# An RMS norm that streams 67 MB: the first store to memory takes four rows per partition instead of one

## The chip, the cores and the metric

The kernel runs on one core of a Trainium2 chip, the other cores idle. The metric is the device time of one execution in microseconds (us), lower is better. "The profile" is one execution taken by the hardware profiler. Its span is about 1.8 us shorter than the device time. A run over 1.5% above the fastest of its kernel counts as slow (164.01 of the kernel before is one); ranges list it, ratios leave it out.

## The reference

```python
def reference(x, gamma):                       # x: 16 x 1024 x 512 float32, gamma: 512
    eps = 1e-5
    rms = np.sqrt(np.mean(x ** 2, axis=-1, keepdims=True) + eps)
    return (x / rms * gamma).astype(np.float32)
```

16,384 rows of 512 floats are read, each scaled by its own factor and by gamma, and written: 33.56 MB in, 33.55 MB out.

## The kernel before

The rows are cut into four tiles of 128 partitions x 32 rows. A row is 2 KB, so one partition's rows of a tile are 64 KB, contiguous in memory. Three SBUF slots hold the tiles, and tile 3 reuses slot 0. All transfers are issued by SyncE on one queue, in program order. The parts that matter (cuts are marked):

```python
    load(0, 0, 0, 8)                  # tile, slot, first row, end row
    nc.sync.dma_start(out=gamma_row, in_=gamma.unsqueeze(0))
    load(0, 0, 8, 16)
    load(0, 0, 16, 32)
    load(1, 1, 0, 16)
    load(1, 1, 16, 32)
    # ... (cut)
    groups = [
        (0, 0, 7, (7,), 3),           # tile, first row, rows, pieces of the square sums, POOL's share
        (0, 7, 9, (9,), 5),
        (0, 16, 16, (7, 9), 7),
        # ... (cut)
    ]
    # ... (cut)
    def transfers(t, g):              # called after each group
        if (t, g) == (0, 0):
            store(0, 0, 0, 1)         # the early store: the program's first
            load(2, 2, 0, 20)
        elif (t, g) == (0, 16):
            load(2, 2, 20, 32)
            store(0, 0, 1, 16)
            store(0, 0, 16, 32)
            load(3, 0, 0, 16)         # slot 0 again: waits for the stores of its rows
            load(3, 0, 16, 32)
        # ... (cut): store(1, 1, 0, 32), store(2, 2, 0, 32), store(3, 0, 0, 32)
```

In each group POOL scales its share of the rows and multiplies them by gamma. ACT and DVE do the same for the other rows.

## Time and profile before

| | before |
|---|---|
| device time, median (lowest to highest), 3 runs | 161.67 us (161.36 to 164.01) |
| span of the profile | 159.7 us |
| busy DVE / ACT / POOL | 70% / 67% / 69% |
| DMA packets' time, as a share of 16 engines' span | 98.1% |
| data packets per DMA engine in the early store | 8 of 2 KB |

Here the DMA share is full and no compute engine is, which means that the transfers set the time, as long as the next transfer is always issued before the last one has ended.

The trace records each DMA packet's duration, though no view prints it. Packets of one size nearly all take the same time (1213 ns for 32 KB), but just before some turns from loads to stores, some load packets take longer, up to 2.3 us. (The first loads are stretched too, in the first 6 us; that belongs to no turn, and is left out.) The stretch of a turn is the sum of each packet's duration minus the median of its size, over the packets around the turn, divided by 16 engines. It is known to a few hundredths of a us, since where "around" ends is a choice.

### The profile page before, as it was taken

What the parts mean: (1) busy time and instruction counts of PE and PEld (TensorE: products, weight loads), DVE (VectorE), ACT (ScalarE), POOL (GpSimd) and SP (SyncE); (2) the same over time, 40 slices, a digit from 0 to 9 for tenths busy, and PEclk for the clock granted to TensorE, in tenths of its full rate; (3) what the DMA queues carried; (4) which work ended last, traced back from release to release, by engine and by line L of the source; (5) the groups of instructions that cost most, each with busy time, mean ns of one, the idle gap of its engine ahead of it and who ended that gap; (6) DMA issues with size and microseconds to landing.
All of it is one profiled execution on the core that took longest, in us unless ns stands there. A gap on an engine that the chain in (4) does not pass through costs nothing.

```text
span 159.7 us, 260 instructions
## 1 busy us (share of the span) xinstructions
PE 2.0 (1%) x2; PEld 0.5 (0%) x2; DVE 111.0 (70%) x40; ACT 106.6 (67%) x106; POOL 110.3 (69%) x24
## 2 busy tenths in 40 slices
PE   0040000000000000000000000000000000000000
PEld 0000000000000000000000000000000000000000
DVE  0018098899798999999999999999999094000000
ACT  3071967976999998999899899989960970000000
POOL 1000951994999599999999999999999999000000
DMA  6999999999999899989999999996996996997993
GB/s 195 415 439 464 460 394 419 492 402 394 402 451 492 361 412 425 492 378 451 468 394 419 501 394 394 525 509 279 525 509 279 525 509 279 525 460 328 525 394 131
DMA packets 2164, 67.12 MB, mean 420 GB/s; under 512 B 242, under 2 KB 242, under 8 KB 371
## 3 DMA queue, kind: packets, MB, share of 16 engines
q1 hardware_dynamic: 2162, 67.11, 98.1%
q14 instruction: 2, 0.01, 0.0%
HBM read 33.56 MB, written 33.55 MB: 420 GB/s over the span
## 4 chain that ended last, share of the span: by engine, by line
POOL 46%; ACT 18%; DVE 12%; DMA 5%; POOLq 4%; issue 0%
POOL slot L108 24%; POOL slot L107 22%; DVE ss L95 9%; ACT slot L94 7%; ACT sq_psum L94 6%; DMA slot<-in_x_dram 5%; POOLq L203 4%; ACT slot L116 3%; DVE slot L120 3%; ACT ss L100 1%; ACT gamma_b L158 0%; DVE ss L101 0%; POOLq L107 0%
## 5 line engine op out<-in xcount | busy, mean ns | idle before, releaser
L107 POOL TENSOR_TENSOR slot<-slot,ss 128x3584 f32<-128x3584 f32 (+2 forms) x9 | 48.6, 5404 | 24.0 <-DVE ss L101 24.0
L108 POOL TENSOR_TENSOR slot<-slot,gamma_b 128x3584 f32<-128x3584 f32 (+2 forms) x9 | 61.4, 6825 | 0.7
L95 DVE TENSOR_REDUCE ss<-sq_psum 128x7 f32<-128x3584 f32 (+1 forms) x13 | 42.2, 3246 | 13.5 <-ACT sq_psum L94 13.5
L116 ACT ACTIVATE slot<-slot,ss 128x512 f32<-128x512 f32 x73 | 46.0, 707 | 4.7 <-DVE ss L101 4.7
L120 DVE TENSOR_TENSOR slot<-slot,gamma_psum 128x4608 f32<-128x4608 f32 (+3 forms) x10 | 40.3, 4038 | 4.4 <-ACT slot L116 4.4
L94 ACT ACTIVATE sq_psum<-slot 128x3584 f32<-128x3584 f32 (+1 forms) x13 | 34.6, 2659 | 6.2 <-DMA slot<-in_x_dram 5.5
L95 DVE TENSOR_REDUCE ss<-slot 128x9 f32<-128x4608 f32 x3 | 14.9, 4953 | 4.4 <-ACT slot L94 4.2
L95 DVE TENSOR_REDUCE ss<-sq_sbuf 128x5 f32<-128x2560 f32 x5 | 14.0, 2801 | 0.0
L94 ACT ACTIVATE slot<-slot 128x4608 f32<-128x4608 f32 x3 | 12.1, 4033 | 0.0
L94 ACT ACTIVATE sq_sbuf<-slot 128x2560 f32<-128x2560 f32 x5 | 11.6, 2322 | 0.0
L100 ACT ACTIVATE ss<-ss,eps_t 128x16 f32<-128x16 f32 (+2 forms) x9 | 2.7, 305 | 11.9 <-DVE ss L95 11.9
L101 DVE RECIPROCAL ss<-ss 128x16 f32<-128x16 f32 (+2 forms) x9 | 2.1, 235 | 0.4 <-ACT ss L100 0.4
L64 PE MATMUL gamma_psum<-gamma_row,ones_col 1*128 1x512 f32 x2 | 2.0, 1121 | 7.9 <-DMA gamma_row<-in_gamma_dram 7.9
L70 ACT ACT_TABLE_LOAD x1 | 1.3, 1283 | 1.1 <-PEq L192 1.1
L158 ACT COPY gamma_b<-gamma_psum 128x512 f32<-128x512 f32 x1 | 0.6, 566 | 0.0
L64 PEld LDWEIGHTS gamma_psum<-gamma_row,ones_col 1*128 1x128 f32 x2 | 0.5, 304 | 7.8 <-issue 7.8
L62 POOL MEMSET ones_col<- 1x128 f32 x1 | 0.2, 194 | 0.3 <-POOLq L192 0.3
L192 POOL MEMSET const-float32-0.0<- 128x1 f32 x1 | 0.1, 98 | 0.2 <-issue 0.2
L70 ACT ACTIVATE table<-eps_t 128x1 f32<-128x1 f32 x1 | 0.2, 203 | 0.0
L192 POOL MEMSET const-bfloat16-1.0<- 128x1 bf16 x1 | 0.1, 101 | 0.0
L192 POOL MEMSET const-uint8-127<- 128x1 uint8 x1 | 0.1, 101 | 0.0
L192 POOL MEMSET const-float32-1.0<- 128x1 f32 x1 | 0.1, 98 | 0.0
(1 smaller groups left out, 0.1 us busy)
## 6 DMA issues: line engine op xcount, KB each, us to landing
slot<-in_x_dram SPq DMA_DIRECT2D x5, 4096.0 KB, 20.8
slot<-in_x_dram SPq DMA_DIRECT2D x1, 5120.0 KB, 27.7
slot<-in_x_dram SPq DMA_DIRECT2D x2, 2048.0 KB, 9.4
out_dram<-slot SPq DMA_DIRECT2D x1, 4096.0 KB, 26.5
out_dram<-slot SPq DMA_DIRECT2D x1, 3840.0 KB
slot<-in_x_dram SPq DMA_DIRECT2D x1, 3072.0 KB, 12.9
out_dram<-slot SPq DMA_DIRECT2D x1, 256.0 KB, 15.9
out_dram<-slot SPq DMA_DIRECT2D x3, 28.1
```

Of the source, the lines that this page charges most:

```text
L64: nc.tensor.matmul(gamma_psum[:, 0], ones_col, gamma_row, start=True, stop=True)
L70: nc.scalar.activation(out=table, in_=eps_t, func=AF.Sqrt)
L94: nc.scalar.activation(out=sq[:, :m], in_=rows, func=AF.Square)
L95: nc.vector.tensor_reduce(out=ss[:, r : r + m, 0], in_=sq[:, :m], axis=mybir.AxisListType.X, op=OP.add)
L100: nc.scalar.activation(out=ss[:, :n, 0], in_=ss[:, :n, 0], func=AF.Sqrt, bias=eps_t, scale=1.0 / D)
L101: nc.vector.reciprocal(out=ss[:, :n, 0], in_=ss[:, :n, 0])
L107: nc.gpsimd.tensor_tensor(out=part, in0=part, in1=by_row, op=OP.mult)
L108: last = nc.gpsimd.tensor_tensor(out=part, in0=part, in1=gamma_b.to_broadcast([P, share, D]), op=OP.mult)
L116: nc.scalar.activation(out=x[:, g + r, :], in_=x[:, g + r, :], func=AF.Copy, scale=rstd[:, r])
L120: scaled = nc.vector.tensor_tensor(out=part, in0=part, in1=gamma_psum.to_broadcast([P, r1 - r0, D]), op=OP.mult)
L158: nc.scalar.copy(out=gamma_b[:, 0], in_=gamma_psum[:, 0])
L203: with _tile.TileContext(nc) as tc:
```

## The change

The early store takes rows 0 to 3 of each partition instead of row 0 alone, 1 MB instead of 256 KB, and the later one takes the rest. The intent is that finished rows leave sooner, in packets of 8 KB instead of 2 KB.

```diff
         if (t, g) == (0, 0):
-            store(0, 0, 0, 1)
+            store(0, 0, 0, 4)
             load(2, 2, 0, 20)
         elif (t, g) == (0, 16):
             load(2, 2, 20, 32)
-            store(0, 0, 1, 16)
+            store(0, 0, 4, 16)
             store(0, 0, 16, 32)
```

## The prediction

> **What bounds the kernel now.** The kernel normalises 16,384 rows of 512 floats: four tiles, t = 0 to 3, each of 32 rows for every one of the 128 partitions, in three SBUF slots (tile 3 reuses slot 0). I read the page's busy shares first, then its queue part.
>
> ```profile
> span 159.7 us, 260 instructions
> PE 2.0 (1%) x2; PEld 0.5 (0%) x2; DVE 111.0 (70%) x40; ACT 106.6 (67%) x106; POOL 110.3 (69%) x24
> ...
> q1 hardware_dynamic: 2162, 67.11, 98.1%
> ```
>
> Three engines are near 70%, none full. The last line is queue, packets, MB, share of the 16 DMA engines' span: their packets fill 98.1% of it. The other 1.9% of 159.7 is 3.0 us, and half of that is the start: in the stretches view the first 5 us have a DMA share of 0.68, so 5 x 0.32 = 1.6 us. Everything is read once and written once (33.56 + 33.55 MB), so the DMA queue sets the end.
>
> The page's "chain that ended last" names POOL for 46%. That is misleading here: the merged chain ends in a last piece of 5.64 us from 129.86, so at 135.5 us, which is the wait for the last multiplication before the last store can be issued; 24 us of pure transfer follow. Whether that chain matters depends on whether the queue is empty at 135.5. So I next read when transfers are issued, in the timeline of the issuing engine, and their times to landing, in the view of each tensor, narrowed to a short window about each issue.
>
> ```profile
> 0.74 0.38 SPq L45 DMA_DIRECT2D slot<-in_x_dram  x1
> 1.18 0.32 SPq L55 DMA_DIRECT2D gamma_row<-in_gamma_dram  x1
> 1.55 2.10 SPq L45 DMA_DIRECT2D slot<-in_x_dram  x4
> 27.19 0.35 SPq L49 DMA_DIRECT2D out_dram<-slot  x1
> 27.58 22.42 SPq L45 DMA_DIRECT2D slot<-in_x_dram  x2
> 50.12 5.46 SPq L49 DMA_DIRECT2D out_dram<-slot  x2
> 71.64 10.41 SPq L45 DMA_DIRECT2D slot<-in_x_dram  x2
> 83.47 52.39 SPq L49 DMA_DIRECT2D out_dram<-slot  x3
> ```
>
> The store at 27.19 is the one that changes. Issue plus time to landing gives the queue's schedule. The first five loads land by 42.5 (3.2 + 39.3); the early store at 43.1 (27.2 + 15.9); tile 2's first 20 rows at 55.3 (27.6 + 27.7); its last 12, issued at 49.7, at 62.6; the store of rows 1 to 15 at about 71.6, since the load that waits for it goes out at 71.64; the store of rows 16 to 31 at 81.7; tile 3's two loads at 91.0 and 100.9; the three big stores at 120.3, 139.6 and 158.9. At every issue something earlier has not landed yet. The backlog is 42.5 - 27.2 = 15.3 us at the early store, 55.3 - 49.7 = 5.6 at tile 2's second load, 81.7 - 71.6 = 10.1 at tile 3's first, 120.3 - 111.5 = 8.8 at the store of tile 2, and 139.6 - 135.5 = 4.1 at the last store. The queue never runs dry.
>
> **What the Trainium skill says.** "DMA: Bandwidth & Descriptors", section "Queues, rings and completion order", says that each engine takes its descriptors in ring order. The landings above agree: they follow issue order. Its section "Why small descriptors are slow (HBM only)" gives each packet a fixed cost of about 3 cycles, so short packets waste more. The trace's packet records let me measure that here: the duration is 84 ns for 2,048 B, 608 for 16,384, 912 for 24,576, 1138 for 30,720, 1213 for 32,768 and 2418 for 65,536 (medians). The slope is (2418 - 1213) / 32,768 = 0.0368 ns per byte, and 84 - 75 leaves about 9 ns per packet. Its section "Specifications" puts the least size for line rate at 512 B; the 2 KB packet is above that, and 75 of its 84 ns are moving data, which agrees. "Perfetto Trace Analysis", section "DMA Instruction — HWDGE (DVE, Sync)", says an issue's recorded interval leaves out the data movement, which is why I take times to landing and not the 0.35 us of the issue.
>
> **The change part by part.** (1) The early store grows from one row to four per partition. The instruction count is unchanged, and so is the packet count: one packet per partition, 128 packets, 8 per DMA engine, in either kernel. A packet grows from 2,048 to 8,192 B, by the fit 9 + 8192 x 0.0368 = 310 ns. The early store costs 8 x (310 - 84) = 1.81 us more per engine.
> (2) The later store shrinks from 15 rows to 12: packets of 30,720 become 24,576 B, and tile 2's 12-row load shows what that takes, 912 ns. It costs 8 x (1138 - 912) = 1.81 us less. The sum is zero: 84 + 1138 = 1222 and 310 + 912 = 1222. Same bytes, same number of packets, same number of semaphore increments.
> (3) When can the four rows leave? In the code, group 0 leaves 7 - 3 = 4 rows to ACT and DVE, and one DVE instruction multiplies all four by gamma:
>
> ```profile
> 24.89 2.28 DVE L120 TENSOR_TENSOR slot<-slot,gamma_psum 128x2048 f32<-128x2048 f32 x1
> ...
> 27.19 0.35 SPq L49 DMA_DIRECT2D out_dram<-slot  x1
> 27.58 0.43 SPq L45 DMA_DIRECT2D slot<-in_x_dram  x1
> ```
>
> It writes 2,048 elements, which is four rows, and ends at 27.17; even the one-row store waits for it. Four rows are released at the same moment. Rows 4 to 6 are POOL's; the change stops just short of them. No wait is added.
> (4) What moves is tile 2's loads, now behind 1.81 us more of store: landing at 57.1 instead of 55.3, and 64.4 instead of 62.6. The first square of tile 2 starts at 64.24 and its rows from 16 on are first read at 77.93, so 7.1 and 13.5 us of slack remain. After the smaller store the sums meet again, at 71.6, so tile 3's load is issued and lands as before.
> Sum: 0.0 us on the queue, 0.0 on the compute chain.
>
> **The rivals.** Rival A: the delayed loads of tile 2 become a compute wait. In the waits view the only DMA wait of a computing engine other than PE's for gamma is
>
> ```profile
> ACT sq_psum L94 <- DMA slot<-in_x_dram: 5.5, 1, 5.5
> ```
>
> which is the very first load. With 7.1 us left the rival needs a delay four times mine. Even then, the end would move only by what exceeds the 4.1 us backlog at the last store. It would make 161.6 to 162.
> Rival B: turning the queue from reading to writing has a cost that depends on the packets. In the packet records, the 32 KB load packets just before the early store are stretched beyond 1213 ns by a total of 0.42 us per engine, but at the two later turns from load to store by only 0.10 and 0.08. Two explanations are open: 2 KB packets overlap badly with the loads before them, or the stretch belongs to that moment. If larger packets cure it the kernel gains about 0.3 us (161.3); if more bytes of store make it worse it may lose as much (161.9).
> Rival C: the store of rows 4 to 15 lands later than 71.6, for example by a turn's cost, and tile 3's first load with it. That load lands at 91.0 and its square begins at 91.61, so only 0.6 us are free. But its place in the queue is fixed by a 10.1 us backlog, and a late square would still have 4.1 us before the queue starves at the last store. So nothing at the end: 161.6.
> Rival D: short packets are so bad that the larger ones gain. Against it: the count of packets doesn't change, and at 9 ns fixed per packet even removing all 8 per engine would be 0.07 us.
>
> **Range and chances.** Predicted is 161.6 us, the median of before (161.67) with at most 0.1 taken off for rival B. Rival B spans 161.3 to 161.9; the three runs before lie at 161.36, 161.67 and 164.01, so a median can wander, more upward. The range is 160.9 to 162.5. Faster by 2% means 3.2 us, more than all the idle DMA time of the span (3.0 us), and half of that is the start, which isn't touched: 0.01. Slower by 2% needs a stall of 3.2 us that the queue's backlogs don't cover, or a slow set of runs: 0.02. Within 2%: 0.97.
>
> **What would show it right or wrong.** Right: 98% share for the queue; packets still about 2164, those under 8 KB down from 371 to 243 because the 128 early ones are no longer under it; the early store issued at 27.2 and landing about 1.8 us later than before (near 17.7 us after its issue); tile 2's first load landing about 29.5 us after its issue; tile 3's first load still issued near 71.6; no new ACT wait on a load. Wrong: an issue of the early store later than 27.3 (step 3), an ACT wait near 64 or 91 us (step 4, rivals A and C), a packet of 8 KB well away from 310 ns (step 1), or a gap in the queue. The prediction fails if a stall of the DMA engines appears that the packet sizes don't tell of.

## More of the kernel before

Where a windows line is shown, bytes count where their packet starts. One wave of sixteen 32 KB packets is 131 GB/s in a 4 us window, so only large differences count there.

## The result

| | before | after |
|---|---|---|
| device time, median (lowest to highest), 4 runs each | 161.63 us (161.36 to 164.01) | 162.16 us (162.13 to 162.48) |
| span of the profile | 159.7 us | 160.4 us |
| DMA share x span | 156.7 us | 157.2 us |
| early store: issue to landing | 15.9 us | 18.8 us |
| last store: issue + time to landing | 135.5 + 23.4 = 158.9 | 135.4 + 24.1 = 159.5 |

A ratio is the mean time of one kernel's fast runs over that of the other's fast runs of the same rounds, so it is not quite the ratio of these medians. Here it is 1.0043, with a 95% interval of 1.0023 to 1.0063. The change is within 2%, as predicted, but it is slower, by 0.5 us going by the medians and 0.7 by the ratio, and that is clear of the noise. The page of the changed kernel, then its timeline of the issuing engine (start, duration, engine, line, operation, tensors):

```profile
span 160.4 us, 260 instructions
...
PE 2.0 (1%) x2; PEld 0.5 (0%) x2; DVE 111.0 (69%) x40; ACT 106.6 (66%) x106; POOL 110.3 (69%) x24
...
DMA packets 2163, 67.12 MB, mean 419 GB/s; under 512 B 241, under 2 KB 241, under 8 KB 242
...
q1 hardware_dynamic: 2162, 67.11, 98.0%
```

```profile
27.05 0.35 SPq L49 DMA_DIRECT2D out_dram<-slot  x1
27.44 22.42 SPq L45 DMA_DIRECT2D slot<-in_x_dram  x2
49.97 5.46 SPq L49 DMA_DIRECT2D out_dram<-slot  x2
72.30 10.32 SPq L45 DMA_DIRECT2D slot<-in_x_dram  x2
83.33 52.40 SPq L49 DMA_DIRECT2D out_dram<-slot  x3
```

The compute engines do the same work in the same time. The early store is issued at 27.05, so the four rows were not waited for. The queue is as full as before. What moved is the load at 72.30, which went out at 71.64 before: it waits for the store of rows 4 to 15, and that landed 0.7 us late. The loss is therefore older than 72 us. The waits view shows that the delay reached the compute engines too, and how little:

```profile
ACT sq_psum L94 <- DMA slot<-in_x_dram: 5.6, 2, 5.4
```

There are two waits now instead of one. The second, some 0.3 us in the view of the input tensor, is for tile 3's load at 91.8 us. It is gone again before the last store, which is issued at 135.4 (135.5 before). The view of the output tensor, narrowed to that store, has before

```profile
L49 SPq DMA_DIRECT2D out_dram<-slot x1: 332/332/332, 135.5 to 135.5; - x1
DMA to landing us min/median/max: 23.4/23.4/23.4
```

and after

```profile
L49 SPq DMA_DIRECT2D out_dram<-slot x1: 332/332/332, 135.4 to 135.4; - x1
DMA to landing us min/median/max: 24.1/24.1/24.1
```

So the loss is in the queue. The windows view brackets it. The columns are stretch of time, its length, busy time and instruction count of PE, PEld, DVE, ACT and POOL, TensorE clock, DMA share, GB/s. Before:

```profile
34.00:38.00 4.00, 0.00 (x0) 0.00 (x0) 4.00 (x2) 1.43 (x4) 3.51 (x1) 1.00 1.14 492
38.00:42.00 4.00, 0.00 (x0) 0.00 (x0) 2.94 (x3) 4.00 (x2) 2.25 (x1) 1.00 0.80 291
42.00:46.00 4.00, 0.00 (x0) 0.00 (x0) 3.92 (x2) 4.00 (x4) 3.92 (x2) 1.00 1.25 536
```

After:

```profile
34.00:38.00 4.00, 0.00 (x0) 0.00 (x0) 4.00 (x2) 1.43 (x4) 3.37 (x1) 1.00 1.18 508
38.00:42.00 4.00, 0.00 (x0) 0.00 (x0) 2.93 (x3) 4.00 (x2) 2.40 (x1) 1.00 0.87 262
42.00:46.00 4.00, 0.00 (x0) 0.00 (x0) 3.93 (x2) 4.00 (x4) 3.92 (x2) 1.00 1.00 426
```

Both kernels sag between 38 and 42 us, just before the early store's packets start (the first at 41.6 us before, at 42.2 after). In the next 4 us the kernel before makes up for it (536 GB/s) and the changed one does not (426), though that difference is less than one wave. The packet records give the size:

| stretch per engine, us | near 40 us (early store) | near 60 us (next store) | near 100 us (tile 1's store) |
|---|---|---|---|
| before | 0.46 | 0.12 | 0.09 |
| after | 1.05 | 0.00 | 0.13 |

The sum rises from 0.67 to 1.18, by 0.51 us. The whole time of all packets rises by 0.53 us per engine, and the last store lands about 0.65 us later. Some 0.15 us I can't assign. The early store's own packets do not vary: each lasts 84 ns before and 309 ns after, as the fit said. Only loads ahead of it are stretched, the last two packets of each engine. Why does the size of a store decide how long the loads before it take?

### The profile page after: what moved, and what is told of

The parts are those of the page before. It is cut to its first block, busy times and chain, and to the rows that moved or that the text cites. A ratio compares the mean times of both kernels' runs of the same rounds, so it can differ in the third digit from the quotient of the medians.

```text
span 160.4 us, 260 instructions
## 1 busy us (share of the span) xinstructions
PE 2.0 (1%) x2; PEld 0.5 (0%) x2; DVE 111.0 (69%) x40; ACT 106.6 (66%) x106; POOL 110.3 (69%) x24
## 4 chain that ended last, share of the span: by engine, by line
POOL 46%; ACT 17%; DVE 12%; DMA 5%; POOLq 4%; issue 0%
POOL slot L108 24%; POOL slot L107 22%; DVE ss L95 9%; ACT slot L94 7%; ACT sq_psum L94 6%; DMA slot<-in_x_dram 5%; POOLq L203 4%; ACT slot L116 3%; DVE slot L120 3%; ACT ss L100 1%; ACT gamma_b L158 0%; DVE ss L101 0%; POOLq L107 0%
## 5 line engine op out<-in xcount | busy, mean ns | idle before, releaser
L95 DVE TENSOR_REDUCE ss<-sq_psum 128x7 f32<-128x3584 f32 (+1 forms) x13 | 42.2, 3247 | 13.4 <-ACT sq_psum L94 13.4
## 6 DMA issues: line engine op xcount, KB each, us to landing
slot<-in_x_dram SPq DMA_DIRECT2D x1, 5120.0 KB, 30.2
out_dram<-slot SPq DMA_DIRECT2D x1, 1024.0 KB, 18.8
```

The lines of the kernel that those rows point to most:

```text
L95: nc.vector.tensor_reduce(out=ss[:, r : r + m, 0], in_=sq[:, :m], axis=mybir.AxisListType.X, op=OP.add)
```

## The experiments

At first I held that a short store between two loads costs by its bytes (theory "bytes"). The rivals were that packet size decides, and that the loss belongs to the moment, for example to compute traffic at 40 us. The first four runs shared one chip and eleven runs of the kernel before, whose median was 161.65 us.

**No early store.** From before:

```diff
-            store(0, 0, 0, 1)
...
-            store(0, 0, 1, 16)
+            store(0, 0, 0, 16)
```

> No early store; all 16 rows leave in the later store. In the packet records the 32 KB load packets just before the early store are stretched by 0.46 us per DMA engine with one row and by 1.05 us with four. If a short store between two loads is what costs (theory: the stretch is caused by the early store and grows with it), that stretch falls to 0.1 us or less and the time is about 0.4 us under before (161.2). If the stretch belongs to that moment (rival: compute traffic at 38 to 42 us), it stays at 0.46 and the time is that of before (161.6).

Measured: 161.84 us (161.80 to 162.23, 6 runs), ratio 1.0017 (1.0004 to 1.0029), no gain. The windows view of this run:

```profile
38.00:42.00 4.00, 0.00 (x0) 0.00 (x0) 2.93 (x3) 4.00 (x2) 2.30 (x1) 1.00 1.01 434
```

The sag at 38 to 42 us is gone (434 GB/s, stretch 0.00) with the same compute beside it, so the moment is not to blame. But the expected 0.4 us did not come: the stretch reappeared near 60 us, 0.87 us, at the turn that cost 0.12 in the kernel before and nothing in the changed one. The same turn, after the same loads, costs that much only where no store has gone before it. Both my theory and its rival fall. The new theory, "paid once", is that the first sizeable store of the program costs about a microsecond, wherever it is. (The traces behind this are one for each kernel, and two for the kernels before and after.)

**Two rows early; seven rows early.** From before, with 1 replaced by 2 and by 7:

```diff
-            store(0, 0, 0, 1)
+            store(0, 0, 0, 2)        # 7 in the other run
...
-            store(0, 0, 1, 16)
+            store(0, 0, 2, 16)       # 7 in the other run
```

> Two rows per partition early, 4 KB packets. If the stretch grows with the bytes stored early, the line through one row (0.46) and four rows (1.05) gives 0.46 + 0.20 = 0.66 us of stretch and about 161.8 us. If four rows merely fall on another alignment by chance, or if there is a threshold between 2 KB and 8 KB packets, the stretch is 0.46 or 1.05.

> Seven rows per partition early, 14 KB packets; rows 4 to 6 are POOL's and done at 22.2 us, so the issue stays at 27.2. If the stretch grows with the bytes: 0.46 + 6 x 0.197 = 1.64 us of stretch and about 162.8 us. If it saturates, or if long packets are what makes the later turns cheap: 1.0 us or less, 162.2 or under.

Measured: two rows 162.11 us (161.71 to 162.41), stretch 1.08. Seven rows 162.41 us (162.25 to 164.25; two of six runs are near 164, as single runs of other kernels are), stretch 0.95. The line through one and four rows was wrong: with two rows the full cost is already there, and with seven it is no more.

**Four rows as four stores of one row.** From after:

```diff
-            store(0, 0, 0, 4)
+            for r in range(4):
+                store(0, 0, r, r + 1)
```

> The same four rows early as in the changed kernel, as four stores of one row: 2 KB packets, 32 per DMA engine instead of 8 of 8 KB, and three more semaphore increments per engine. If the bytes stored early make the stretch: 1.05 us, about 162.2 us plus 24 x 9 ns = 0.2 for the extra packets. If the size of a packet makes it: 0.46 us of stretch and 161.8 with the extra packets.

Measured: 162.61 us (162.58 to 162.82), ratio 1.0062 (1.0050 to 1.0074), stretch 0.94 on the loads ahead of the 2 KB packets. So packet size is not it: a run of 32 small packets costs what 8 larger ones do. Of the 0.45 us over the changed kernel, 24 x 9 ns = 0.2 us are packets, as expected, and 0.1 us is stretch of the small stores' own last packets at 44 us; the rest is not assigned.

Now "paid once" was to be tested: let something else be the first store. The next four runs shared a chip, with 161.50 us for the kernel before. Two of its eleven runs there, at 162.92 and 163.58, widen the intervals of the ratios to 0.5% each way, so for these four I quote medians and stretches. Each queues a store of zeros behind the second load. The right values overwrite them later.

**A first store of one row per partition, then the changed kernel.** From after:

```diff
     load(0, 0, 8, 16)
+    nc.gpsimd.memset(slots[2][:, 0], 0.0)
+    nc.sync.dma_start(out=ov[3][:, 31], in_=slots[2][:, 0])
```

> The changed kernel with one more store of one row per partition (zeros, to the last row of tile 3, which the right values overwrite at the end) queued behind the second load, so that it is the program's first store. New theory: the stretch of some 1 us falls on the last loads before the first store of the program, wherever that is, and later turns are nearly free. Then a stretch of about 0.5 us appears near 13 us and the one at 38 to 42 us falls from 1.05 to about 0.1; the time is 162.15 + 0.67 for the 8 extra packets, - 0.95 + 0.5: about 162.4. Rival: each short store between loads stretches the loads before it; then the stretch at 42 us stays at 1.05 and the time is about 163.3.

Measured: 162.34 us (162.22 to 164.68), stretch 0.23 near 12 us and 0.61 near 40. Neither number was foreseen. The four-row store still pays, but 0.61 instead of 1.05. Less the 0.67 us of added packets, the time would be 161.67, near the 161.50 of the kernel before. One row pays in part.

**A tiny first store.** 16 partitions of 512 B, one packet per engine, to tile 3 and to tile 0, both before the changed kernel, and to tile 3 before the kernel of before:

```diff
     load(0, 0, 8, 16)
+    warm = const.tile([16, 128], fp32)
+    nc.gpsimd.memset(warm, 0.0)
+    nc.sync.dma_start(out=ov[3][0:16, 31, 0:128], in_=warm)   # ov[0][0:16, 0, 0:128] in the second
```

> As the run with the extra row, but the first store is tiny: 16 partitions of 512 B, one packet per DMA engine. If a single packet is enough to pay for the first turn, and pays little since it is small, the stretch at 42 us is about 0.1, and the time about 161.3. If what is paid goes with the bytes, the stretch at 42 us stays near 1.0 and the time is about 162.2.

> The same tiny first store, to the first row of tile 0 (the memory that the early store writes later) instead of the last row of tile 3. If what costs at the first turn goes with the addresses written, this run is faster than the one to tile 3 (161.3 against 162.2); if it goes with the DMA engines alone, the two are the same.

> The kernel before (one row early) with the same tiny first store to tile 3. If a tiny store pays for the first turn, the stretch at 42 us falls from 0.46 to about 0.1 and that at 62 us from 0.12 to 0, and the time is about 161.2, the best of all; if not, 161.7.

Measured: 162.03, 162.10 and 161.64 us, with stretches near 40 us of 1.09, 1.18 and 0.17. The third has a further 0.55 near 60. A tiny store buys nothing, to either address. In the third the sum (0.72) is near that of the kernel before (0.58 at these two turns), but it is divided otherwise. That raised the question whether the stretches repeat at all.

The last four runs shared a chip, with 161.41 us for the kernel before.

**Both kernels again**, unchanged:

> The kernel before again, for a second trace: how far do the stretches repeat? Theory (the first sizeable store of the program costs, a one-row store pays part of it): 0.46 near 40 us and 0.12 near 60 us in the first trace; the sum should again be 0.5 to 0.75, perhaps divided otherwise, as in the run of before with a tiny store (0.17 and 0.55). Rival (the stretch is chance from execution to execution): any value from 0.1 to 1.1. Time 161.6.

> The changed kernel again, for a second trace, and timed on the same chip as the rest. Theory: again 1.0 to 1.2 us of stretch near 40 us, under 0.05 near 60 us, and 162.15 us. Rival (chance): any value.

Measured: before 161.50 us (161.37 to 162.84), stretches 0.33 and 0.37. After 162.13 us (161.93 to 162.30), ratio 1.0041 (1.0029 to 1.0053), stretches 1.25 and 0.00. The loss repeats on another chip session. How a one-row store divides its share between the two turns is chance, while the sum (0.58, 0.70, and 0.72 with the tiny store) stays well under that of the changed kernel (1.05, 1.25).

**A first store as large as the early one.** From after:

```diff
     load(0, 0, 8, 16)
+    nc.gpsimd.memset(slots[2][:, 0:4], 0.0)
+    nc.sync.dma_start(out=ov[3][:, 28:32], in_=slots[2][:, 0:4])
```

> The changed kernel with a first store as large as its own early one, four rows per partition of zeros to tile 3, behind the second load. Theory (paid once, at the first store, if it is large enough): 0.8 to 1.0 us of stretch near 12 us and under 0.1 near 40 us; time 162.15 + 8 x 0.309 = 164.6 us. Rival (every short store between loads stretches them): 1.0 near 12 us and 1.0 near 40 us again, 165.6.

Measured: 164.82 us (164.73 to 164.92), ratio 1.0208 (1.0194 to 1.0221), nearest to the 164.6 of "paid once" and far from the rival's 165.6. The windows view, the kernel before first, then two lines of this run. The new store pushes the queue back by 2.6 us: the early store's first packet starts at 44.8 us instead of 42.2, so 41 to 45 us is the window to hold against 38 to 42.

```profile
10.00:14.00 4.00, 0.00 (x0) 0.00 (x0) 2.65 (x1) 1.31 (x1) 0.00 (x0) 1.00 1.10 471
```

```profile
10.00:14.00 4.00, 0.26 (x1) 0.00 (x0) 2.76 (x1) 1.20 (x1) 0.00 (x0) 1.00 0.92 266
41.00:45.00 4.00, 0.00 (x0) 0.00 (x0) 2.98 (x1) 4.00 (x2) 3.97 (x1) 1.00 0.94 406
```

This run decides between these two theories. Around the new first store the queue moves only 266 GB/s at 10 to 14 us (471 in the kernel before), and the sag before the early store is gone (406 GB/s, against 262 in the changed kernel): 1.19 us of stretch near 12 us, then 0.01 around the very same four-row store that cost 1.05 and 1.25. The first store came from another slot and went to another tile's memory, so the cost is not tied to the addresses either.

**One row, then three more a little later.** From before:

```diff
             load(2, 2, 0, 20)
+            store(0, 0, 1, 4)
...
-            store(0, 0, 1, 16)
+            store(0, 0, 4, 16)
```

> The one-row store as before, then three more rows behind tile 2's first load, then twelve. Theory (a one-row first store pays a smaller part, and the next store pays what is left, little): stretches as before, some 0.46 near 40 us and 0.1 to 0.5 near 54 us, nothing near 62; 161.6 to 161.8. Rival (any early store of several rows stretches the loads by about 1 us): a further 1.0 near 54 us, 162.3 or more.

Measured: 161.70 us (161.47 to 162.41), ratio 1.0022 (1.0005 to 1.0038), stretches 0.20 near 40 us, 0.62 near 53 and nothing at 62. The time is as "paid once" had it and far from the rival's 162.3. The second part was larger than the 0.1 to 0.5 that I allowed. With one row ahead, the same four rows leave before tile 2's second load at a sum of 0.82, not 1.05 to 1.25.

No run beat the kernel before. The stretches of all traces, by the turns in order:

| first store | near 12 us | near 40 us | 53 to 61 us | median, us |
|---|---|---|---|---|
| one row (before; again) | | 0.46; 0.33 | 0.12; 0.37 | 161.63; 161.50 |
| four rows (after; again) | | 1.05; 1.25 | 0.00; 0.00 | 162.16; 162.13 |
| none early, then 16 | | 0.00 | 0.87 | 161.84 |
| two rows | | 1.08 | 0.00 | 162.11 |
| seven rows | | 0.95 | 0.03 | 162.41 |
| four stores of one row | | 0.94 | 0.03 | 162.61 |
| one row of zeros, then four | 0.23 | 0.61 | 0.00 | 162.34, 0.67 of it added packets |
| four rows of zeros, then four | 1.19 | 0.01 | 0.02 | 164.82, 2.47 of it added packets |
| one row, then three | | 0.20 | 0.62 | 161.70 |

## Why the prediction was right, and where its sum was off

**The bound and the backlog** held. The queue's share is 98.0%, no issue was late, and the last store was issued at the same time.

**Parts 1 and 2** (bytes and packets cancel) held exactly as far as they went: 309 ns for 8 KB against 310 predicted, 912 for 24 KB, and 242 packets under 8 KB against 243.

**Part 3** (four rows are released at the moment of one) held: the issue was at 27.05.

**Part 4** was off in its times, not in its consequence. Tile 2's first load landed 30.2 us after issue, not 29.5, and the early store 18.8, not 17.7. The load of tile 3 went out at 72.3, not "as before" at 71.6. The first and the third are about the 0.6 us of stretch added ahead of them. The early store landed 0.95 us later than predicted, at 45.84 us instead of 44.89. Of that, 0.3 us lies after its last packet has ended (0.7 us from there to the landing, 0.4 before), and no run tells why.

**The sum "0.0 us on the queue"** is the step that failed, and the prediction's own last sign of being wrong came true: a stall of the DMA engines that the packet sizes don't tell of. (So did a smaller one, the ACT wait near 91 us.) The sum left out the turn from loads to stores, which I had measured and filed as rival B with "about 0.3 us" either way. Rival B was the right place with the wrong size and the wrong reason. The term is +0.5 us (1.05 + 0.00 + 0.13 against 0.46 + 0.12 + 0.09), and it is neither the overlap of 2 KB packets nor the moment, the two readings that I offered. I called the later turns cheap and looked for the difference in the packets, but the difference was that they were later. A first store of one row happens to pay less than a larger one. That 162.16 us still lies in the range of 160.9 to 162.5 is partly luck: the most that a rival foresaw was 161.9 to 162, and the rest was room left for medians that wander. (One reading was off without consequence: the median of a 16,384 B packet is 611 ns, not 608.)

**Rival A** (a compute wait for tile 2) did not come. **Rival C** came as described: the load of tile 3 was late, a wait of about 0.3 us appeared near 91 us, and the backlog hid it. **Rival D** stands refuted by the split store, where small packets cost their 9 ns each and some stretch of their own, and no more. The 2% bound on both sides was never near.

**What stays open:** what the one-off cost is physically, and why a one-row first store lowers the total to between 0.58 and 0.84 us where two to seven rows pay 0.94 to 1.25. The records show loads that last longer; they don't show why. One rival is left: that loads are stretched where the DMA engines run in step, and that paying once drives them apart. I take as a measure of step the time within which the sixteen packets of one wave start, a few packets before a turn. Much fits the rival. The free turn near 40 us, after four rows of zeros, has the widest waves of that turn (0.69 us, against 0.42 with seven rows and 0.55 in the kernel before). Near 60 us the turns that cost 0.12 to 0.87 have 0.33 to 0.49, and all free ones but one have 0.56 or more. But step alone does not decide. In the run with one row of zeros the turn near 60 us has 0.41 and is free, while a turn near 40 us with 0.39 pays 1.18 (tiny store to tile 0). Two rows have 0.59 and pay 1.08. So it is shown that a large store ahead takes the cost away from a later one; by what means is not.

## What to carry to other kernels

Where a queue is full from start to end, as here at 98%, do not expect moving bytes earlier within it to gain anything by itself. What changed the time here was the packets that lasted longer than their size tells. Look at the packet durations before turns from loads to stores, and do not take the cost of a later turn for that of the first. Where such a cost moves instead of vanishing when its supposed cause is removed, ask what is first there.

## What the Trainium skill lacked or had wrong

- No page tells of a one-off cost at the first sizeable store behind a queue of loads: here 0.94 to 1.25 us per DMA engine for two to seven rows, 0.87 where that store comes at 60 us, and 0.01 for a four-row store once another four-row store has gone before it. It would belong to "DMA: Bandwidth & Descriptors".
- "DMA: Bandwidth & Descriptors", section "Rules for kernel authors", asks for 128 partitions and at least 1 MiB per DMA for the most bandwidth. For one block of bytes the runs agree: four stores of 256 KB in place of one of 1 MB made the kernel 0.45 us slower. But the rule alone misleads about this change: the early store grew from 256 KB to 1 MB, the later one shrank by as much, and the kernel became 0.5 us slower.
